# A joined transformer kernel: norm sums, rotation and gate bias moved off GpSimd, rotary tables made earlier, attention issued in steps

## The chip, the cores and the metric

One core of one Trainium2 chip runs the whole program. The metric is device time in microseconds (us) for one execution. Three runs of the kernel before took 2554.97 to 2559.99 us, median 2557.75 us.

## The reference

Two blocks are joined, on one sequence of 512 tokens of width 1024. Block 1 puts 16 meta tokens ahead (528 rows) and runs a gated feed-forward (width 2816), a hybrid mixer, and a second feed-forward. Block 2 runs a recurrent mixer ("hy": an RG-LRU beside an mLSTM in chunks), a convolutional feed-forward (width 3072), a gated embedding ("ple"), then sliding-window attention with rotary positions ("swa"), again a convolutional feed-forward and ple. Each part begins with an RMS norm.

```python
def hybrid_mixer(u, ...):
    sb_q, sb_k, sb_v, c_q, c_kv, k_r, gate_pre = jnp.split(up @ w_in, idx, axis=-1)
    y_sb = from_heads(stick_breaking_attention(sb_q, sb_k, sb_v)) @ w_sb_o   # 8 heads of 64
    q = einsum(rmsnorm(c_q, q_norm_g), w_uq); kv = einsum(rmsnorm(c_kv, kv_norm_g), w_ukv)
    y_mla = from_heads(latent_attention(q_nope, q_rope, k_nope, k_rope, v, cid)) @ w_mla_o
    g = sigmoid(gate_pre + b_gate)
    return (g_sb * y_sb + g_mla * y_mla) @ w_out

def stick_breaking_attention(q, k, v):       # per block of 128 queries
    z = q @ k.T * scale
    log_1m = where(strict, log_sigmoid(-z), 0); csum = cumsum(log_1m)
    a = where(strict, exp(log_sigmoid(z) + csum[..., -1:] - csum), 0)
    return a @ v

def rglru_mlstm_mixer(h, ...):
    y_rg = rg_lru(causal_dwconv(x_rg), ...) * gelu(g_rg)
    q, k = split(silu(causal_dwconv(concat([q, k]))))
    y_ml = sigmoid(o) * rms_norm(mlstm_chunkwise(q, k, v, i_pre, f_pre))
    return concat([y_rg, y_ml]) @ w_out
```

## The kernel before

Activations lie transposed, features on the 128 partitions and tokens along the free side. Every linear layer keeps float32 accuracy by splitting both operands into a high and a low part of type fp32r: `wload` (L280) fetches a weight block of up to 128x1024, ScalarE casts it (`whi`, L286), VectorE subtracts to get the rest (`wlo`, L287), and `mm` (L295 to L302) issues three matmuls per 128 rows, high x high, high x low and low x high. A block of 1024 rows and 512 tokens is thus 24 matmuls of 128x512; these stand at L301 (with L314 for token-major products and L328 for the first products behind a norm). Such a matmul is called a dense matmul below.

A list scheduler sets the order of each engine's instructions, from the order of the code, its priorities (`high_priority`) and its own estimates; each engine then works through its list in order, and the tiles' dependences become semaphore waits. PSUM in the attention stages has four banks for scores (`z`), two for linear layers (`l`) and two for transposes and outputs (`a`).

The mixer of block 1 has two attentions of 8 heads. `stick` (L681) works in four rounds c of two heads: projections of the next round's q and k (`proj`), four gate blocks (`gates`, 96 dense matmuls), and four query blocks b of 128. For each: scores (L717 for two heads at once, L677 for one) plus a mask product with a bf16 identity (L719, L679), a chain of softplus, running sum and exp on ScalarE and VectorE, transposes of the probabilities (L642) and the products with V (L653, `attn_pv`). In L653 each head fills 64 of the 128 output columns, so two heads lie side by side; the last 16 keys are a product of their own with 16 rows. Gates get their bias on GpSimd (L701). `latent` (L751) has the same form with ordinary softmax; its projections are smaller, and the output product of the first attention (`wo`, 96 dense matmuls) follows at its end. Then `mixer` adds the two gated branches on GpSimd (L616), splits and multiplies with `wout`.

`norm` (L388) sums the squares of 8 feature blocks; with `dense=True` all on VectorE, else blocks 1 to 5 on GpSimd (L412). Five norms are not dense: norm_ffn0, norm_ple0, norm_mix1, norm_ffn1 and norm_ple1.

In `hy` (L863) the z of q and k are convolved (L929 to L933), then the gate rows `gts` are scanned and transposed (L956), `weights` (L961) builds the decay matrix of a head from a row sent through DRAM, multiplies it with a causal mask on GpSimd and with q k products (L973, L974), `heads` (L977) makes the head's output, and `rglru` (L1014) runs in the same loop. The output product `hyo` follows with all 8 row blocks.

In `swa` (L1161) `tables` (L1129) computes cosine and sine from the positions at the start, and `norm(g)` in it normalizes and rotates q and k: per half one product with the cosine (`ra`) on VectorE and one with the sine (`rb`) on GpSimd (L1229), and their sum or difference.

Of the kernel before, what the change touches and what calls it, by code (L numbers as in the profile page):

```python
# [15 lines left out]
P = 128  # L16
# [56 lines left out]
def prep(inp):  # L73
# [31 lines left out]
    r["hyo"] = _wt(a["hy_w_out_2"][0].reshape(KD, P, D)[[4, 5, 0, 1, 2, 3, 6, 7]].reshape(D, D))  # L105
# [110 lines left out]
class Kern:  # L216
# [63 lines left out]
    def wload(self, src, n):  # L280
# [4 lines left out]
        with self.tc.high_priority(offset=100):  # L285
# [31 lines left out]
    def lin_first(self, srcs, x, kc, c0=0, wide=False, two=False, k0=0):  # L317
# [12 lines left out]
        return [e if two else e[0][0] for _, e in out]  # L330

# [56 lines left out]
    def norm(self, hs, gname, tt, side, upd=None, tb=P, dense=False):  # L388
# [58 lines left out]
    def begin(self, st):  # L447
# [9 lines left out]
        self.per = self.pool(st, "per")  # L457
        self.pdram = [self.tc.dram_tile([P, KD, T], F32, name=f"pd{l}") for l in range(2)]
# [11 lines left out]
    def ffn(self, n, h, tt, name):  # L470
# [24 lines left out]
        for gi, fh in enumerate((8, 7, 7)):  # L495
# [26 lines left out]
            f0 += fh  # L522
        return self.post(fs, half, hs, tt)

    def mixer(self, n, h):
# [15 lines left out]
        with ExitStack() as stS:  # L541
            S = self.pool(stS, "S")
            vt = S.tile([P, 5, 512], F32, name="sbv")
            with ExitStack() as st:
# [53 lines left out]
            self.stick(S, x, n.rs, vt, ysb, masks[:, :P], gs, gm)  # L598
        n.st.close()
        n.st = ExitStack()  # L600
        for m in range(0, KD, 2):
            self.act(gs[:, m:m + 2, :], gs[:, m:m + 2, :], AF.Sigmoid)
            self.act(gm[:, m:m + 2, :], gm[:, m:m + 2, :], AF.Sigmoid)
        O = self.pool(n.st, "O1")
        ymla = [O.tile([P, 4, T], F32R, name=nm) for nm in ("ymh", "yml")]
        with ExitStack() as st:
            self.latent(st, cq, ckv, kr, masks[:, P:], ymla, ysb, gs)
# [21 lines left out]
    def attn_pv(self, pool, probs, c, nb, vt, ydst, b):  # L629

        nc = self.nc
        hp = ExitStack()
        hp.enter_context(self.tc.high_priority(offset=100))
        slots = [(i, hh) for i in range(nb) for hh in range(2)] + [(nb, hh) for hh in range(2)]
        where = {}
        for g0 in range(0, len(slots), 4):
            grp = slots[g0:g0 + 4]
            pt = self.sbank()
            at = pool.tile([P, 512], F32, name="at", bufs=3)
            for j, (i, hh) in enumerate(grp):  # L640
                kk = P if i < nb else META
                nc.tensor.transpose(pt[:kk, j * P:(j + 1) * P], probs[hh][:, i * P:i * P + kk], self.ident)  # L642
                where[(i, hh)] = at[:kk, j * P:(j + 1) * P]
            n1 = sum(1 for i, hh in grp if i < nb)
            if n1:
                (nc.vector.tensor_copy if (g0 // 4) % 2 else nc.scalar.copy)(at[:, :n1 * P], pt[:, :n1 * P])
            if n1 < len(grp):
                nc.vector.tensor_copy(at[:META, n1 * P:len(grp) * P], pt[:META, n1 * P:len(grp) * P])
        po = self.sbank()[:, :P]
        for i in range(nb + 1):  # L650
            kk = P if i < nb else META
            for hh in range(2):
                nc.tensor.matmul(po[64 * hh:64 * hh + 64, :], vt[:kk, i, (2 * c + hh) * 64:(2 * c + hh + 1) * 64],  # L653
                                 where[(i, hh)], start=i == 0, stop=i == nb)
        sl = slice(b * P, (b + 1) * P)
        nc.scalar.copy(ydst[0][:, c, sl], po)
        self.tt(ydst[1][:, c, sl], po, ydst[0][:, c, sl], ALU.subtract)
        hp.close()

    def units(self):  # L660

        for b in range(4):
            n = META + (b + 1) * P
            for heads in (((0, 1),) if n <= 272 else ((0,), (1,))):
                z = self.psp["z"].tile([P, 2, 512], F32, name="z", tag="z")
                if n <= 512:
                    yield b, heads, n, z[:, :len(heads), :n], [[(z[:, i, :n], 0, n)] for i in range(len(heads))]
                else:
                    w = n // 2
                    yield b, heads, n, z[:, :, :w], [[(z[:, s, :w], s * w, (s + 1) * w) for s in range(2)]]  # L670

    def scores(self, pieces, q, k, mask):

        nc = self.nc
        for i, (ps, a, b) in enumerate(pieces):
            last = i == len(pieces) - 1
            nc.tensor.matmul(ps, q, k[:, a:b], start=True, stop=not last)  # L677
            if last:
                nc.tensor.matmul(ps[:, b - a - P:], self.idb, mask, start=False, stop=True)  # L679

    def stick(self, S, x, rs, vt, ysb, mask, gs, gm):  # L681
# [3 lines left out]
        qk = {}  # L685

        def proj(c):
            q = S.tile([P, T], F32, name="sbq", bufs=2)
            k = S.tile([P, TM], F32, name="sbk", bufs=2)
            ps = self.lin1(d["sbq"][c], x, KD, META)  # L690
            nc.vector.scalar_tensor_tensor(q, ps, 0.125, rs[:, META:], op0=mul, op1=mul)
# [704 lines left out]
```

## Time and profile before

| what | value |
|---|---|
| profiled execution's own time | 2557.62 us |
| its span, mean granted clock | 2555.8 us, 0.997 |
| PE busy / weight loads | 2516.6 us (98%) / 2085.1 us (82%) |
| VectorE / ScalarE / GpSimd busy | 1363.4 (53%) / 974.4 (38%) / 238.4 us (9%) |
| PE on the chain that ended last | 91% |
| DMA | 239.42 MB, mean 94 GB/s |

PE's matmuls are pipelined: a row of the profile shows how long one was in flight, and the next begins before it ends. The pace is read from the distance between the starts, or from the count of matmuls in a stretch. A busy share near 100% can therefore hide a slow pace.

### The profile page before, as it was taken

Reading aid. Unit: us, or ns where it says so; the run is one execution under the profiler, and the core shown is the slowest. Engines: PE = TensorE matmul, PEld = TensorE weight load, DVE = VectorE, ACT = ScalarE, POOL = GpSimd, SP = SyncE. Lnnn points to the kernel's source line nnn. Section 1 sums busy time; section 2 is a strip of 40 time slices with the busy share of each in tenths; the row PEclk is TensorE's granted clock in tenths of the full one; section 3 lists DMA queues with packets and bytes.
Section 4 is the critical chain, followed back from the end, with each engine's and each line's share of the span. In section 5 each row is a group of like instructions: output and inputs, shape, how many; then the busy total and the mean of one; then the engine's idle time right before and its main releaser. Section 6 shows DMA issues by size and latency. Waiting matters only on the chain.

```text
span 2555.8 us, 33215 instructions
## 1 busy us (share of the span) xinstructions
PE 2516.6 (98%) x13328; PEld 2085.1 (82%) x13334; DVE 1363.4 (53%) x2167; ACT 974.4 (38%) x1561; POOL 238.4 (9%) x207
## 2 busy tenths in 40 slices
PE   8999999999999999999999999999999999999999
PEld 8999998767767888888777788888888568888887
DVE  5333347355575542344688655355475776535544
ACT  4222235343663532223534633223343563322332
POOL 1101100011102010101000111001111011100110
PEclk9999999999999999999999999999999999999999
DMA  4222233211112433233322322332333123233232
GB/s 142 90 89 91 91 100 129 80 57 59 49 36 79 150 106 99 95 100 103 113 83 91 124 93 93 96 107 90 92 109 100 34 67 134 93 95 107 91 92 99
DMA packets 77490, 239.42 MB, mean 94 GB/s; under 512 B 9172, under 2 KB 11476, under 8 KB 77080
## 3 DMA queue, kind: packets, MB, share of 16 engines
q1 hardware_dynamic: 77336, 237.30, 28.6%
q8 instruction: 105, 1.72, 0.3%
q14 instruction: 49, 0.40, 0.0%
HBM read 225.72 MB, written 8.40 MB: 92 GB/s over the span
## 4 chain that ended last, share of the span: by engine, by line
PE 91%; DVE 4%; ACT 2%; issue 1%; DMA 1%; POOL 1%; SPq 0%; DVEq 0%; POOLq 0%; ACTq 0%
PE l L301 77%; PE l L328 5%; PE a L653 2%; PE z L677 1%; PE l L314 1%; PE a L642 1%; PE s L1302 1%; PE a L382 1%; DVE wlo L287 1%; PE a L367 1%; POOL gm L247 0%; ACT whi L286 0%; ACT e L236 0%; PE a L1330 0%; PE a L1324 0%
## 5 line engine op out<-in xcount | busy, mean ns | idle before, releaser
L286 ACT CAST whi<-wraw 128x1024 fp32r<-128x1024 f32 (+4 forms) x448 | 432.0, 965 | 1090.9 <-PE l L301 889.2
L301 PE MATMUL l<-xh,whi 128*128 128x512 f32 (+3 forms) x2368 | 786.0, 358 | 0.5 <-DVE sbk L247 0.5
L301 PE MATMUL l<-xl,whi 128*128 128x512 f32 (+3 forms) x2368 | 782.0, 356 | 0.0
L301 PE MATMUL l<-xh,wlo 128*128 128x512 f32 (+3 forms) x2368 | 781.7, 356 | 0.0
L287 DVE TENSOR_TENSOR wlo<-wraw,whi 128x1024 fp32r<-128x1024 f32 (+4 forms) x448 | 502.0, 1121 | 274.0 <-ACT whi L286 265.3
L301 PEld LDWEIGHTS l<-xh,whi 128*128 128x128 f32 (+1 forms) x2368 | 421.6, 188 | 67.2 <-issue 5.5
L301 PEld LDWEIGHTS l<-xh,wlo 128*128 128x128 f32 (+1 forms) x2368 | 420.8, 188 | 64.2 <-issue 2.6
L301 PEld LDWEIGHTS l<-xl,whi 128*128 128x128 f32 (+1 forms) x2368 | 421.4, 188 | 63.0 <-issue 2.5
L301 PE MATMUL l<-chh,whi 128*128 128x512 f32 x384 | 149.4, 389 | 0.0
L301 PE MATMUL l<-chl,whi 128*128 128x512 f32 x384 | 149.4, 389 | 0.0
L301 PE MATMUL l<-chh,wlo 128*128 128x512 f32 x384 | 149.4, 389 | 0.0
L301 PE MATMUL l<-hh,wlo 128*128 128x256 f32 (+2 forms) x528 | 140.1, 320 | 0.0
L301 PE MATMUL l<-hh,whi 128*128 128x256 f32 (+2 forms) x528 | 140.0, 319 | 0.0
L301 PE MATMUL l<-hl,whi 128*128 128x256 f32 (+2 forms) x528 | 139.8, 319 | 0.0
L247 POOL TENSOR_TENSOR t<-g,xrs 128x528 f32<-128x528 f32 (+1 forms) x44 | 75.7, 1722 | 634.5 <-ACT g L236 634.5
L247 POOL TENSOR_TENSOR cc<-cc,xrs 128x512 f32<-128x512 f32 x48 | 62.8, 1309 | 602.9 <-ACT cc L236 602.9
L247 DVE TENSOR_TENSOR t<-l,t 128x256 f32<-128x256 f32 (+1 forms) x66 | 32.3, 516 | 147.4 <-PE l L301 143.5
L247 DVE TENSOR_TENSOR g<-l,xrs 128x256 f32<-128x256 f32 (+1 forms) x66 | 32.3, 516 | 118.7 <-PE l L301 114.7
L301 PEld LDWEIGHTS l<-hh,whi 128*128 128x128 f32 x528 | 88.3, 188 | 6.8
L301 PEld LDWEIGHTS l<-hl,whi 128*128 128x128 f32 x528 | 88.1, 188 | 6.9
L301 PEld LDWEIGHTS l<-hh,wlo 128*128 128x128 f32 x528 | 88.1, 188 | 6.9
L247 DVE TENSOR_TENSOR cz<-l,xrs 128x512 f32<-128x512 f32 x48 | 33.2, 692 | 110.0 <-PE l L301 105.5
(341 smaller groups left out, 3192.9 us busy)
## 6 DMA issues: line engine op xcount, KB each, us to landing
wraw<-in_up SPq DMA_DIRECT2D x96, 512.0 KB, 3.4
wraw<-in_dn SPq DMA_DIRECT2D x64, 384.0 KB, 3.1
wraw<-in_ffn_g SPq DMA_DIRECT2D x44, 512.0 KB, 3.4
wraw<-in_ffn_u SPq DMA_DIRECT2D x44, 512.0 KB, 3.4
wraw<-in_ffn_d SPq DMA_DIRECT2D x32, 448.0 KB, 3.2
wraw<-in_hy SPq DMA_DIRECT2D x20, 512.0 KB, 3.5
wraw<-in_ffn_d SPq DMA_DIRECT2D x16, 512.0 KB, 3.4
wraw<-in_gate SPq DMA_DIRECT2D x16, 512.0 KB, 3.4
```

Of the source, the lines that this page charges most:

```text
L247: return (eng or self.nc.vector).tensor_tensor(out, a, b, op=op)
L286: nc.scalar.copy(hi, raw)
L287: nc.vector.tensor_tensor(lo, raw, hi, op=ALU.subtract)
L301: self.nc.tensor.matmul(ps, a[:, k * m:(k + 1) * m], b[:, k0 + k, c0:c1], start=first and k == 0 and pi == 0, stop=last and k == kc - 1 an ...
L314: self.nc.tensor.matmul(ps[:c1 - c0, :n], a[:, k, c0:c1], b[:, j * n:(j + 1) * n], start=k == 0 and pi == 0, stop=k == nk - 1 and pi == 2)
L328: self.nc.tensor.matmul(ps, a[:, k * P:(k + 1) * P], b[:, k0 + k, t0:t1], start=k == 0 and pi == 0, stop=k == kc - 1 and pi == 2)
L367: nc.tensor.matmul(ps[:w, i * 64:(i + 1) * 64], acc[:, c:c + w], self.ones[:, :64], start=True, stop=True)
L382: nc.tensor.matmul(p[:, c - a:c - a + w], r[:w, i:i + 1].to_broadcast([w, P]), self.ident[:w, :w], start=True, stop=True)
L642: nc.tensor.transpose(pt[:kk, j * P:(j + 1) * P], probs[hh][:, i * P:i * P + kk], self.ident)
L653: nc.tensor.matmul(po[64 * hh:64 * hh + 64, :], vt[:kk, i, (2 * c + hh) * 64:(2 * c + hh + 1) * 64], where[(i, hh)], start=i == 0, stop=i ...
L677: nc.tensor.matmul(ps, q, k[:, a:b], start=True, stop=not last)
L1302: nc.tensor.matmul(z[:, i * n:(i + 1) * n], qt[r, 2 * g + i, b * P:(b + 1) * P], kt[r, g, k0:k0 + n], start=False, stop=i == 1)
```

## The change

Linear layers in the two attentions become generators (`step_lin`) which yield after each of a block's dense products, and a loop (`fill`) hands out a set number of them between the parts of an attention; transposes (`attn_t`) and V products (`attn_v`) become two calls with fills between; the last 16 keys lie in a zeroed tile of 128 rows, so that their V product has 128 rows too; scores of two heads are issued in turn; `wo` of the first attention goes into the second. Five norms sum wholly on VectorE, the gates' bias goes into ScalarE's Sigmoid, the last three branch sums and the rotation's `rb` go to VectorE. The rotary tables are made in the second feed-forward, written to DRAM and read in `swa`. In `hy` the gates' scan and `rglru` come before `weights`, first taps and biases go to ScalarE, and `hyo` is two products of four row blocks, the first of them issued between the heads.

```diff
+    def step_lin(self, src, x, kc, done, c0=0, two=False):
+        hi, lo = self.wload(src, kc * P, 2000)
+        segs, ev = self.banks2() if two else self.banks1(c0)
+        for k in range(kc):
+            for pi, (a, b) in enumerate(((hi, x[0]), (hi, x[1]), (lo, x[0]))):
+                for ps, t0, t1 in segs:
+                    self.nc.tensor.matmul(ps, a[:, k * P:(k + 1) * P], b[:, k, t0:t1],
+                                          start=k == 0 and pi == 0, stop=k == kc - 1 and pi == 2)
+                yield
+        with self.tc.high_priority(offset=1000):
+            done(ev)
...
-                self.tt(acc, acc, sq, ALU.add, None if dense or k > KD - 3 else nc.gpsimd)
+                self.tt(acc, acc, sq, ALU.add)
...
+            if not two and gi == 0:
+                with ExitStack() as st:
+                    self.tables(self.pool(st, "trg", side=self.other))
...
-            self.act(gs[:, m:m + 2, :], gs[:, m:m + 2, :], AF.Sigmoid)
+                self.act(g[:, m, :], g[:, m, :], AF.Sigmoid, bias=self.v("b_gate", b + m))
...
-            self.tt(gm[:, m, :], gm[:, m, :], gs[:, m, :], add, nc.gpsimd)
+            self.tt(gm[:, m, :], gm[:, m, :], gs[:, m, :], add, nc.gpsimd if m < 5 else None)
...
+    def last_keys(self, pt, o, probs, nb, rest, where):
+        for hh in range(2):
+            self.nc.tensor.transpose(pt[:META, o + hh * P:o + (hh + 1) * P], probs[hh][:, nb * P:nb * P + META], self.ident)
+            where[(nb, hh)] = rest[:, hh * P:(hh + 1) * P]
+        self.nc.vector.tensor_copy(rest[:META, :], pt[:META, o:o + 2 * P])
...
+        for row in zip(*todo):
+            for hh, (ps, a, b), last in row:
+                nc.tensor.matmul(ps, q(hh), k(hh)[:, a:b], start=True, stop=not last)
...
+        for c in range(4):
+            ng = (3, 4, 4, 5)[c]
+            self.todo = ([proj(c + 1)] if c < 3 else []) + [gates.pop(0) for _ in range(ng)]
+            if c == 0:
+                self.fill(8)
+            probs = start(c, 0)
+            if late:
+                self.attn_v(*late)
+            self.fill(12)
+            for b in range(4):
+                if b < 3:
+                    nxt = start(c, b + 1)
+                    self.fill((14, 18, 22)[b])
+                else:
+                    self.fill(24 * ng + (48 if c < 3 else 0) - (8 if c == 0 else 0) - 102)
+                t = self.attn_t(S, probs, c, b + 1, vt, ysb, b, rest[b % 2])
+                self.fill(6)
...
+        for i, c in enumerate((0, 4, 1, 5, 2, 6, 3, 7)):
+            z = z_of(8 + c)
+            t = R.tile([P, T], F32, name="t", bufs=2)
+            self.conv(t, z, [self.v(f"mlc{j}", c) for j in range(4)])
+            self.act(qk[:, c, :], t, AF.Silu, bias=self.v("mlcb", c))
+            if i % 2:
+                rglru(i // 2)
...
+            if hd > 1:
+                for m in range(4 * hd - 8, 4 * hd - 4):
+                    out(m)
...
-                self.tt(b, xs[1 - s_], sin, mul, nc.gpsimd)
+                self.tt(b, xs[1 - s_], sin, mul)
```

PE in the first attention before, round c = 0, last query block (L642 transposes of the probabilities `e`, L653 products with V, L301 dense matmuls of the gates):

```order
L642 MATMUL a<-cst,e 16x128
L301 MATMUL l<-xh,whi 128x512
L301 MATMUL l<-xl,whi 128x512
L301 MATMUL l<-xh,wlo 128x512
L653 MATMUL a<-at,sbv 64x128
L301 MATMUL l<-xh,whi 128x512
L653 MATMUL a<-at,sbv 64x128
L301 MATMUL l<-xl,whi 128x512
L653 MATMUL a<-at,sbv 64x128
L301 MATMUL l<-xh,wlo 128x512
```

The same block after, round c = 1 (L343 dense, L672 and L684 transposes, L695 V products, `rest` the zeroed tile of the last keys):

```order
L672 MATMUL a<-cst,e 128x128 x6
L343 MATMUL l<-xl,whi 128x512
L343 MATMUL l<-xh,wlo 128x512
L684 MATMUL a<-cst,e 16x128 x2
L343 MATMUL l<-xh,whi 128x512
L695 MATMUL a<-at,sbv 64x128 x8
L695 MATMUL a<-rest_4907,sbv 64x128 x2
L343 MATMUL l<-xl,whi 128x512
```

The ten V products, which stood one by one between dense matmuls in rounds 0 and 1, stand in one row in every round.

PE in `hy` before, from the second transpose of the gate rows to the first decay products (L314 dense, L973 products of q and k):

```order
L314 MATMUL l<-whi,xh 128x512
L956 MATMUL a<-cst,gts 128x4 x4
L314 MATMUL l<-whi,xl 128x512
L314 MATMUL l<-wlo,xh 128x512
...
L973 MATMUL l<-qk 128x512
L973 MATMUL l<-qk 128x384
L973 MATMUL l<-qk 128x256
L973 MATMUL l<-qk 128x128
```

And after (L1075 the transposes, L1090 the products):

```order
L301 MATMUL l<-xh,wlo 128x512
L1075 MATMUL a<-cst,gts 128x4 x8
L314 MATMUL l<-whi,xh 128x512
L314 MATMUL l<-whi,xl 128x512
...
L1090 MATMUL l<-qk 128x512
L1090 MATMUL l<-qk 128x384
L1090 MATMUL l<-qk 128x256
L1090 MATMUL l<-qk 128x128
```

Between the transposes and the first q k product there were 8 dense matmuls, and there are 96 now.

VectorE in `swa`, rotation of the last query group, before (`x` the normalized halves, L1224; `rb` is GpSimd's):

```order
L1224 SCALAR_TENSOR_TENSOR x_16451<-a,vecs,x_16451 128x512
L1224 SCALAR_TENSOR_TENSOR x_16533<-a,vecs,x_16533 128x512
L247 TENSOR_TENSOR ra_16657<-x_16451,trig 128x512
L247 TENSOR_TENSOR ra_16666<-x_16533,trig 128x512
L247 TENSOR_TENSOR ra_16657<-ra_16657,rb_16658 128x512
L247 TENSOR_TENSOR ra_16666<-ra_16666,rb_16667 128x512
```

And after:

```order
L1336 SCALAR_TENSOR_TENSOR x_16509<-a,vecs,x_16509 128x512
L1336 SCALAR_TENSOR_TENSOR x_16591<-a,vecs,x_16591 128x512
L247 TENSOR_TENSOR ra_16715<-x_16509,trig 128x512
L247 TENSOR_TENSOR rb_16716<-x_16591,trig 128x512
L247 TENSOR_TENSOR ra_16724<-x_16591,trig 128x512
L247 TENSOR_TENSOR ra_16715<-ra_16715,rb_16716 128x512
L247 TENSOR_TENSOR rb_16725<-x_16509,trig 128x512
```

The two sine products now stand in VectorE's own list.

## Rows read from the trace of the kernel before

**Rows 1.** Stretches: us, each engine's busy us (instructions), PE clock, DMA share, GB/s
```profile
27.00:398.00 371.00, 371.00 (x3050) 371.00 (x3049) 141.47 (x212) 108.47 (x143) 37.90 (x26) 1.00 0.29 92
501.96:608.86 106.90, 106.67 (x563) 74.47 (x562) 58.44 (x91) 42.55 (x77) 11.43 (x23) 1.00 0.18 60
608.86:683.62 74.76, 74.53 (x416) 51.39 (x415) 49.69 (x80) 46.05 (x81) 11.20 (x20) 1.00 0.16 51
702.93:782.33 79.40, 78.50 (x552) 53.25 (x550) 55.77 (x163) 47.32 (x129) 0.00 (x0) 1.00 0.10 32
900.00:1238.00 338.00, 338.00 (x1494) 279.73 (x1493) 134.98 (x153) 106.67 (x134) 38.12 (x23) 1.00 0.31 100
```
**Rows 2.** The same for the dense matmuls of L301 alone
```profile
501.96:608.86 106.90, 79.77 (x337) 55.78 (x336) 1.00 0.18 60
608.86:683.62 74.76, 51.15 (x193) 34.38 (x192) 1.00 0.16 51
702.93:782.33 79.40, 27.22 (x104) 16.47 (x102) 1.00 0.10 32
```
**Rows 3.** Timeline of PE, round 1: start, us in flight, then what
```profile
588.66 0.43 PE L653 MATMUL a<-at,sbv 128*64 128x128 f32 x2
589.02 0.50 PE L301 MATMUL l<-xh,whi 128*128 128x512 f32 x1
589.45 0.43 PE L653 MATMUL a<-at,sbv 128*64 128x128 f32 x2
```
**Rows 4.** Timeline of PE, round 2
```profile
635.74 1.46 PE L653 MATMUL a<-at,sbv 128*64 128x128 f32 x20
637.13 0.50 PE L301 MATMUL l<-xl,whi 128*128 128x512 f32 x1
```
**Rows 5.** Timeline of PE, round 0, first query block
```profile
508.14 0.44 PE L653 MATMUL a<-at,sbv 128*64 128x128 f32 x4
508.51 0.50 PE L301 MATMUL l<-xh,whi 128*128 128x512 f32 x1
```
**Rows 6.** Timeline of PE, scores of two heads, then of one
```profile
556.25 0.73 PE L717 MATMUL z<-sbk,sbq 64*128 64x272 f32 x4
556.91 0.28 PE L719 MATMUL z<-masks,idb 128*128 128x128 bf16 x2
...
560.21 0.92 PE L677 MATMUL z<-sbk,sbq 64*128 64x400 f32 x2
561.06 0.33 PE L642 MATMUL a<-cst,e 128*128 128x128 f32 x1
```
**Rows 7.** Waits of PE's weight loads, 684 to 783: us in total, times, longest
```profile
PEld a L653 <- ACT at L646: 2.8, 7, 0.6
```
**Rows 8.** Waits of PE, 1340 to 1440
```profile
PE l L973 <- DVE s L974: 2.8, 1, 2.8
PE l L328 <- ACT xh L291: 2.3, 1, 2.3
PE a L1003 <- DVE nm L1002: 2.3, 3, 1.4
PE a L956 <- DVE gts L247: 0.7, 1, 0.7
```
**Rows 9.** Waits of PE, 783 to 880
```profile
PE l L328 <- ACT ooh L291: 2.1, 1, 2.1
```
**Rows 10.** Groups of GpSimd and VectorE by form: busy us, mean ns, idle before
```profile
L247 POOL TENSOR_TENSOR acc<-acc,sq 128x512 f32<-128x512 f32 x25 | 35.6, 1424 | 237.6 <-ACT sq L226 237.6
L247 POOL TENSOR_TENSOR gm<-gm,gs 128x512 f32<-128x512 f32 x8 | 14.7, 1832 | 128.9 <-DVE gm L247 128.9
L287 DVE TENSOR_TENSOR wlo<-wraw,whi 128x1024 fp32r<-128x1024 f32 x306 | 376.0, 1230 | 188.6 <-ACT whi L286 185.2
L247 DVE TENSOR_TENSOR ra<-x,trig 128x512 f32<-128x512 f32 x10 | 14.9, 1518 | 0.0
L247 DVE TENSOR_TENSOR ra<-ra,rb 128x512 f32<-128x512 f32 x10 | 6.4, 679 | 0.0
```

More of the change, by code (lines that the diff above doesn't have):

```diff
@@ L627, in mixer, with attn_t @@
         return h, upd
-    def attn_pv(self, pool, probs, c, nb, vt, ydst, b):
+    def attn_t(self, pool, probs, c, nb, vt, ydst, b, rest):
         nc = self.nc
-        hp = ExitStack()
-        hp.enter_context(self.tc.high_priority(offset=100))
-        slots = [(i, hh) for i in range(nb) for hh in range(2)] + [(nb, hh) for hh in range(2)]
+        slots = [(i, hh) for i in range(nb) for hh in range(2)]
         where = {}
[L636 to L670, printed above, removed]
@@ L672, in scores @@
-    def scores(self, pieces, q, k, mask):
-        nc = self.nc
[L675 to L679, printed above, removed]
+        with self.tc.high_priority(offset=100):
+            for g0 in range(0, len(slots), 4):
+                grp = slots[g0:g0 + 4]
+                pt = self.sbank()
+                at = pool.tile([P, 512], F32, name="at", bufs=3)
+                for j, (i, hh) in enumerate(grp):
+                    nc.tensor.transpose(pt[:, j * P:(j + 1) * P], probs[hh][:, i * P:(i + 1) * P], self.ident)
+                    where[(i, hh)] = at[:, j * P:(j + 1) * P]
+                n1 = len(grp) * P
+                if n1 <= 256:
+                    self.last_keys(pt, 256, probs, nb, rest, where)
+                (nc.vector.tensor_copy if (g0 // 4) % 2 else nc.scalar.copy)(at[:, :n1], pt[:, :n1])
+            if nb % 2 == 0:
+                self.last_keys(self.sbank(), 0, probs, nb, rest, where)
@@ L792, in proj, with qdone @@
-            return qk
-        nxt = proj(0)
-        late = None
-        for c in range(4):
-            qk = nxt
-            if c < 3:
-                nxt = proj(c + 1)
+                    yield from self.step_lin(d["uq"][4 + 2 * j + c // 2], cq, 3, turn(j))
+            qk[c] = [[], []]
+            def qdone(ev):
+                for hh in range(2):
+                    q = L.tile([96, T], F32, name=f"q{hh}", bufs=2)
+                    self.copy(q[:64], ev[0][0][64 * hh:64 * hh + 64])
+                    i = 2 * (c % 2) + hh
+                    self.tt(q[64:96], t12[32 * i:32 * i + 32, 0, :], t12[32 * i:32 * i + 32, 1, :], add)
+                    qk[c][hh].append(q)
@@ new lines, in kdone, with wo, done @@
+            def kdone(ev):
+                for hh in range(2):
+                    k = L.tile([96, TM], F32, name=f"k{hh}", bufs=2)
+                    for p, s in ev:
+                        self.copy(s(k[:64]), p[64 * hh:64 * hh + 64])
+                    self.copy(k[64:96], kr)
+                    qk[c][hh].append(k)
+            yield from self.step_lin(d["uq"][c], cq, 3, qdone)
+            yield from self.step_lin(d["uk"][c], ckv, 2, kdone, two=True)
+        def wo(m):
+            def done(ev):
+                self.tt(gs[:, m, :], ev[0][0], gs[:, m, :], mul)
+            yield from self.step_lin(d["wo"][m][:, :512], ysb, 4, done)
@@ L937, in hy @@
             self.act(sq[:, c, :], sq[:, c, :], AF.Sqrt, bias=tiny)
+        for c in range(4):
+            self.act(rr[:, c, :], rr[:, c, :], AF.Exp, scale=sl[:, c, 1:2])
         L = R2.tile([4, T], F32, name="lf")
```

281 lines of the change are left out of this document (166 added, 115 removed).

## The prediction

> **What bounds the kernel now.** I read the shares of the page first: PE is busy 98% of the span and carries 91% of the chain that ended last, so only PE's list counts, and other engines only where PE waits for them. A busy share says nothing of the pace, so next I compared stretches by PE's count. In the dense stretch 900 to 1238 there are 1494 matmuls in 338 us, 0.226 us each; in 27 to 398, where they have half the width (256 or 272), 3050 in 371 us, 0.1216 each [rows 1]. All feed-forwards run at this pace and the change can give nothing there. The two attentions don't. In rounds 0 and 1 of the first (501.96 to 608.86) L301 has 337 matmuls [rows 2], by the code 240 whole and 97 half ones: 240 x 0.226 + 97 x 0.1216 = 66.1 us. The other 40.8 of 106.9 us are the attention's own products and what they cost around them. Rounds 2 and 3 have 193 whole ones, 43.7 us, and 31.1 us besides. The second attention has 104, 72 whole and 32 half: 20.2 us, and 59.2 besides. Together 131 us go there, and `hy` has 8.1 us of waits of PE [rows 8]. That is where I look.
>
> **The change part by part.**
>
> *First attention.* The four rounds have the same attention work, yet 0 and 1 take 40.8 us and 2 and 3 take 31.1. The timeline shows why: in rounds 0 and 1 the ten V products of the last query block stand singly between dense matmuls. One takes 0.36 us from its start to the next start (588.66 to 589.02), and the dense one behind it 0.43 instead of 0.226 [rows 3]; together 0.56 us above the dense pace. In round 2 the same ten stand in one row and take 1.39 us (635.74 to 637.13) [rows 4]. So 10 x 0.56 - 1.39 = 4.2 us are lost in each of two rounds, 8.4 of the 9.7. The order after shows one row of ten in every round. I take 9, between 8.4 and 9.7. The last keys, a product of 16 rows, now have 128 rows and stand in the row of the others. Two V products by themselves take 0.37 us (508.14 to 508.51) [rows 5], ten 1.39, so two in a row of ten 0.28; a joined row saves 0.09 at least, and 0.3 where a dense matmul behind a V product goes too (0.43 against 0.226) [rows 3]. Of 16 blocks that is 1.4 to 4.8; I take 2.5, near the middle since the rows for both are there. Scores of two heads in turn run side by side: four matmuls of 64x272 begin and end within 0.66 us, while one head of 64x400 takes 0.85 [rows 6]. After, the 400-key scores of both heads are neighbours in rounds 1 and 2 and not in 0 and 3, so up to 0.85 each; I take 1.5. Sum 13 us, from 9 (with 4 us given back to new waits) to 16.
>
> *Second attention.* Its products stay. The same 16 joined rows give 2.5 again (1.4 to 4.8). What else can go is waiting: it has few dense matmuls to put between, and V products wait seven times for the copy behind their transposes, 2.8 us [rows 7]. The 96 dense matmuls of `wo`, which stood behind it, now stand between; they cost the same 21.7 us in either place, but cover these waits. I take 2.5 + 2.8 = 5.3, from 1.4 (waits stay) to 9 (waits of the other kinds go as well, at the upper price for the rows).
>
> *Branch sums.* PE waits 2.1 us for the first split behind the last sum [rows 9]. That sum takes 1.83 us on GpSimd; one of that shape takes 0.68 on VectorE [rows 10], so 1.15 goes on the last block, and a little on the two before: 1.5, from 0.5 to 2.1.
>
> *`hy`.* The wait for `s` (2.8) and for the gate rows (0.7) [rows 8] arise where only 8 dense matmuls, 1.8 us, lie between the transposes of the gate rows and the first products of q and k. There are 96 after, 21.7 us: both go. The waits for `nm` (2.3) come where VectorE has `rglru` in its list between the steps of a head; that work is now ahead of the loop: 2.0 goes. The wait for `xh` (2.3) is for the split before `hyo`; the first half of `hyo` now begins with blocks that come from the gelu, behind the same table load on ScalarE, so I give it 1.3. Sum 6.8, from 3 to 8.1. It doubles the loads of `hyo` to 16 halves and adds 8 additions of 0.68 on VectorE, 5.5 us beside some 43 us of dense matmuls: nothing, and 5.5 if that cover failed.
>
> *Rotation.* Per group VectorE now does 2 x 1.518 + 2 x 0.679 = 4.4 us while GpSimd makes `rb` [rows 10]. With `rb` in its own list it has six instructions. If all go at 0.679, that is 4.1, 0.3 less; if `ra` stays at 1.518, 5.8, 1.4 more. The `ra` and the sum have the same shape and differ by 2.2 times, and only `ra` runs beside GpSimd, so I take the first: five groups, 1.0 us (from -7 to 1.6). The Trainium skill (SBUF — State Buffer, Who interferes with whom) says that a VectorE instruction with two inputs in SBUF contends with a GpSimd instruction that reads SBUF; by that rule `ra` falls back to its own duration, and by a plain count of instructions the change would cost 5 x 2 x 0.68 = 6.8 us here. The rows bear out the rule.
>
> *Norm sums and tables.* A norm's five sums take 5 x 1.424 = 7.1 us on GpSimd and 5 x 0.68 = 3.4 on VectorE [rows 10], 3.7 us less, but behind each norm stand 48 dense matmuls or so (10.9 us) that need no scale. That covers four of the norms; at norm_mix1, where the tables' VectorE instructions stood in front too, I take 1.2 (from 0 to 3.7). The tables move into the second feed-forward: VectorE is busy 135 of 338 us there [rows 1], and their 19 instructions are 13 us at 0.68 each. On SP the DMA that writes them waits for the last Sin with weight loads behind it; two blocks are ahead, 48 dense matmuls, 10.9 us. If that were not enough, PE would lose a few us once.
>
> *Gate bias.* Sixteen GpSimd instructions go; nothing waited for them but Sigmoid, which now is 16 instead of 8 instructions, behind the last gates and beside 77 dense matmuls.
>
> **Sum.** 13 + 5.3 + 1.5 + 6.8 + 1.0 + 1.2 = 28.8 us off the profiled execution's own 2557.6 (span 2555.8 and 1.8 around it; the median of the runs is 2557.75): 2528.8 us.
>
> **The rivals.**
>
> *A: new waits where switches go.* In the order after, a row of V products stands one or two dense matmuls (0.2 to 0.45 us) behind its transposes, and the copy lies between. Rows 7 price such a wait at 0.4 us (2.8 over 7). On 32 blocks that is 12.8 us: 2541.6. For it: the copies stay on ScalarE and VectorE, which are more than half busy here [rows 1]. Against: rounds 2 and 3 have the same form already and are the better ones.
>
> *B: everything at its upper price.* 16 + 9 + 2.1 + 8.1 + 1.6 + 3.7 = 40.5: 2517. For it: the stretches have waits that I did not count; against: all of it at once.
>
> *C: slower.* `step_lin` puts its casts 2000 places ahead where 100 were. ScalarE and VectorE work in order, so a cast and a subtraction of 1.23 us [rows 10] can stand ahead of the softmax of each query block, and each cast waits for a buffer that PE frees. If each of 32 blocks comes 1.23 us late with no cover, 39 us are lost: 2568. It decides from 28.8 / 32 = 0.9 us a block. For it: VectorE is busy 55 to 70% in these stretches [rows 1]. Against: before, too, these casts go ahead of the softmax, and 18 to 39 dense matmuls (4 to 9 us) now stand between scores and transposes of the long blocks.
>
> *D: the order hardly changes.* The call that would hold PE's order by hand is not used; the list scheduler may place the pieces as it did. The order after speaks against it in round 1. Then only the last four terms stay, 10.5: 2547.
>
> **How the numbers follow.** Forecast 0.60, A 0.20, B 0.12, C 0.04, D 0.04. The predicted time is the forecast's 2529, its own range 2522 to 2537 (the first two terms at 16 + 9 or at 9 + 1.4). The range for 8 in 10 takes in A and D and most of B, and leaves C out: 2510 to 2547; its lower end stands below B because waits not counted could go too. A measurement of this kernel can tell about 0.2%, 5 us, from no change. Only C ends above, and a worse D inside: faster 0.93, same 0.03, slower 0.04.
>
> **What would show it.** Right: the first attention's rounds each near 14.5 us above their dense matmuls; V products in rows of ten at 1.24 to 1.4 us; no wait for `s` or `gts` in `hy`; `ra` near 0.68 us; dense stretches unchanged to the microsecond. Wrong: transposes or V products that wait 0.4 us and more in every block (A), or whole-microsecond waits of PE for `e` with casts ahead of it on ScalarE (C); a wait of PE behind SP's write of the tables.

## The result, and the profile after

The kernel after takes 2533.09 us (median of 4 runs, 2530.61 to 2533.38) against 2558.69 us before (4 runs, 2554.97 to 2559.99): ratio 0.990, 95% interval 0.9883 to 0.9917. Forecast 2529, range 2510 to 2547. The total is close; the terms that make it up are not.

The page after: the span, and each engine's busy time and instructions.

```profile
span 2531.4 us, 33257 instructions
PE 2496.9 (99%) x13334; PEld 2081.7 (82%) x13334; DVE 1360.7 (54%) x2197; ACT 993.6 (39%) x1601; POOL 162.3 (6%) x159
```

GpSimd lost 76 us of work and ScalarE gained 19. Of the 24.4 us that the span lost, 6.8 are clock: TensorE lost them to half speed in the profile of before (rows below), and after it lost none until the work ended. The runs differ likewise: their granted clock is 0.995 to 0.998 before (all series) and 0.998 to 1.0 after. Where the 24.4 us went is read from the starts of TensorE's matmuls: between the same two products of both traces, the difference of the distances is the gain of that stage.

| stage, by TensorE's products | before, us | after, us | gain | forecast |
|---|---|---|---|---|
| start to the mixer's first norm product of `rc` | 438.04 | 441.13 | -3.10 | 0 |
| to the first product of `wout` (both attentions) | 380.00 | 374.45 | 5.55 | 18.3 |
| to the last product of `wout` (branch sums) | 47.38 | 45.65 | 1.73 | 1.5 |
| to the first product of `pph` behind feed-forward 2, the norm ahead of it with it | 373.65 | 372.08 | 1.57 | 0 |
| to the first down product (`chh`) of convolutional feed-forward 0, with `hy` | 366.19 | 360.98 | 5.21 | 6.8 |
| to its last down product | 260.89 | 260.89 | 0.00 | 0 |
| to the first down product of feed-forward 1, with norms, ple and `swa` | 378.19 | 364.84 | 13.35 | 2.2 |
| the rest | 306.99 | 306.99 | 0.00 | 0 |

Two rows stand out: the attentions gave 13 us less than forecast, `swa` gave 11 us more. The first row is no effect of the change: TensorE's list is the same there in all fourteen kernels, and the twelve below reach that product 0.26 to 3.53 us later than the profile of before did. About 1.1 of the 3.1 us is there by the 200th product. The rest comes from the pace: from 100 to 200 us the profile of before has 824 matmuls and that of after 819, with no wait and the clock at 1.00 in both. Seven of the twelve run at the pace of after and five at that of before; what sets it is open.

The four rounds of the first attention after, then the second attention: each stretch, its length, and busy time and count of the dense matmuls alone (L343; answers to [rows 2]).

```profile
495.34:537.46 42.12, 29.07 (x137) 22.06 (x136) 1.00 0.20 63
537.46:587.52 50.06, 36.70 (x169) 27.98 (x168) 1.00 0.21 64
587.52:637.85 50.33, 36.69 (x169) 27.95 (x168) 1.00 0.21 64
637.85:678.39 40.54, 27.41 (x107) 19.18 (x106) 1.00 0.10 31
699.70:794.88 95.18, 47.79 (x177) 29.42 (x177) 1.00 0.14 42
```

At 0.2262 us for a whole dense matmul and half of it for a half, the rounds stand 16.8, 17.4, 17.7 and 16.6 us above their dense work, where 14.5 each was forecast. Rounds 0 and 1 together fell from 41 to 34, as the regrouped V products promise, but rounds 2 and 3 rose from 31 to 34. The row of ten is as forecast (answer to [rows 3, 4], round 0):

```profile
535.10 1.09 PE L695 MATMUL a<-at,sbv 128*64 128x128 f32 x16
536.02 0.39 PE L695 MATMUL a<-rest,sbv 128*64 128x128 f32 x4
536.34 0.50 PE L343 MATMUL l<-xh,wlo 128*128 128x512 f32 x1
```

Ten products take 1.24 us (535.10 to 536.34), 1.39 before. What rose are the waits. TensorE's waits from 441 to 816 after (line, releaser: us, times, longest):

```profile
PE a L672 <- ACT e L236: 3.9, 9, 0.7
PE l L343 <- ACT q L243: 3.1, 2, 2.4
PE l L343 <- DVE sbk L247: 2.1, 4, 0.6
PE a L672 <- DVE e L894: 1.1, 1, 1.1
```

and the same stretch before, 438 to 818:

```profile
PE l L301 <- ACT q L243: 1.3, 2, 0.7
PE l L765 <- ACT mlav L243: 0.6, 1, 0.6
PE l L301 <- DVE sbk L247: 0.5, 1, 0.5
PE z L677 <- DVE e L739: 0.4, 2, 0.2
```

2.8 us became 10.2 here. Inside the four rounds alone it is 0.4 before and 5.5 after: 3.9 for `e`, ahead of transposes, and 1.6 for `sbk`.

The scores did not run as forecast either. Two heads' products lie side by side when both start at once. The four records of 64x400 of both heads in round 1 (each product leaves two) did not, though they are neighbours in TensorE's list. The first row is the kernel after; the second and third are two kernels from the experiments below, with casts 100 places ahead and with the first attention's order held by hand:

```profile
549.35 1.97 PE L721 MATMUL z<-sbk,sbq 64*128 64x400 f32 x4
547.81 1.49 PE L721 MATMUL z<-sbk,sbq 64*128 64x400 f32 x4
546.72 0.94 PE L721 MATMUL z<-sbk,sbq 64*128 64x400 f32 x4
```

They take 1.90 us to the next start after, 1.42 and 0.87 in the other two. Over the whole first attention the scores take, from each start to the next and without idle time, 21.8 us before, 20.7 after, 17.9 with casts 100 ahead and 12.4 by hand. Why the second head starts late is not shown.

The largest wait, 2.37 us from 688.8 to 691.1, is for the copy of `q` at the start of the second attention, with this ahead of it on ScalarE:

```profile
684.85 3.18 ACT L236 ACTIVATE gm<-gm,vecs 128x512 f32<-128x512 f32 x5
687.94 1.03 ACT L286 CAST whi<-wraw 128x1024 fp32r<-128x1024 f32 x1
688.87 0.72 ACT L236 ACTIVATE gm<-gm,vecs 128x512 f32<-128x512 f32 x1
...
689.90 0.57 ACT L243 COPY q<-l 64x512 f32<-64x512 f32 x1
```

Six of the sixteen Sigmoids stand there.

In `swa` the trace of before holds what the prediction did not look at. TensorE, with the idle time ahead of a row in brackets:

```profile
1968.33 0.39 PE L301 MATMUL l<-xh,wlo 128*128 128x512 f32 x1
1970.35 1.08 PE L1210 MATMUL a<-hsel,ss 128*128 128x64 f32 x8 [1.63 <-DVE ss L247]
...
1972.37 0.63 PE L301 MATMUL l<-xl,whi 128*128 128x512 f32 x1
1972.79 0.63 PE L301 MATMUL l<-xh,wlo 128*128 128x512 f32 x1
```

and VectorE before, just ahead of that wait:

```profile
1965.28 3.12 DVE L247 TENSOR_TENSOR ra<-x,trig 128x512 f32<-128x512 f32 x2
...
1969.52 0.68 DVE L247 TENSOR_TENSOR ss<-ss,sqa 128x512 f32<-128x512 f32 x1
```

`ss`, which TensorE waits for, stands behind the two slow `ra`. A second wait of 1.68 us follows at 1983, for `e`, behind the next `ra`. A third group, for `e` of L1316, was 2.8 us before and is 0.7 after (L1428):

```profile
PE a L1324 <- DVE e L1316: 2.8, 4, 1.2
PE a L1436 <- DVE e L1428: 0.7, 2, 0.5
```

After each of the first two waits dense matmuls start 0.43 us apart instead of 0.227. The granted clock of before (last three columns: clock, DMA share, GB/s) says why:

```profile
865.00:870.00 5.00, 3.04 (x17) 2.45 (x16) 1.83 (x2) 2.29 (x4) 0.00 (x0) 0.96 0.24 72
870.00:875.00 5.00, 5.00 (x21) 4.33 (x21) 2.25 (x5) 1.41 (x4) 0.00 (x0) 0.70 0.28 111
1970.00:1975.00 5.00, 4.65 (x19) 3.87 (x20) 3.53 (x9) 2.24 (x5) 0.00 (x0) 0.71 0.43 105
1975.00:1980.00 5.00, 5.00 (x29) 3.82 (x29) 1.24 (x3) 0.00 (x0) 0.00 (x0) 0.95 0.33 105
1985.00:1990.00 5.00, 4.94 (x14) 2.55 (x14) 4.92 (x16) 2.28 (x9) 0.00 (x0) 0.57 0.37 90
1990.00:1995.00 5.00, 5.00 (x19) 2.98 (x17) 0.94 (x6) 3.74 (x16) 0.00 (x0) 0.74 0.23 68
```

A stretch of 5 us at clock c loses 5 x (1 - c): 1.7 us behind the wait at 868, 1.7 behind that at 1969 and 3.45 behind that at 1983, 6.85 in all, at the lower of the two levels (1.2 instead of 2.4 GHz). After:

```profile
1955.00:1980.00 25.00, 25.00 (x123) 17.64 (x122) 20.04 (x55) 10.42 (x37) 0.00 (x0) 1.00 0.27 74
```

It is 1.00 from 862 to 872 us too. In the trace after the clock falls only in the last 2.2 us, where the work ends. The Trainium skill (TensorE: Matmul & The Clock Gate, Why this matters for your kernels) says that idle gaps of TensorE between bursts of matmuls bring the lower clock back. It speaks of longer gaps than these: in the trace of before the clock falls behind waits of 1.6 to 2.0 us. The rotation after, on VectorE (answer to [rows 10]: `ra` 1518 ns before):

```profile
L247 DVE TENSOR_TENSOR rb<-x,trig 128x512 f32<-128x512 f32 x10 | 6.9, 686 | 0.0
L247 DVE TENSOR_TENSOR ra<-x,trig 128x512 f32<-128x512 f32 x10 | 6.8, 684 | 0.0
```

`hy` after, TensorE's waits from 1233 to 1594 (answers to [rows 8]):

```profile
PE l L328 <- DVE h L247: 1.6, 1, 1.6
PE a L1120 <- DVE nm L1119: 1.0, 3, 0.4
PE l L1090 <- DVE s L1091: 0.4, 1, 0.4
```

### The profile page after: what moved, and what is told of

Its sections match the earlier page's. It is cut to its first block, busy times and chain, and to the rows that moved or that the text cites. A ratio compares the mean times of both kernels' runs of the same rounds, so it can differ in the third digit from the quotient of the medians.

```text
span 2531.4 us, 33257 instructions
## 1 busy us (share of the span) xinstructions
PE 2496.9 (99%) x13334; PEld 2081.7 (82%) x13334; DVE 1360.7 (54%) x2197; ACT 993.6 (39%) x1601; POOL 162.3 (6%) x159
## 4 chain that ended last, share of the span: by engine, by line
PE 91%; DVE 4%; ACT 3%; issue 1%; DMA 1%; POOL 0%; SPq 0%; ACTq 0%; DVEq 0%
PE l L301 71%; PE l L328 5%; PE l L343 5%; PE l L314 2%; PE z L721 1%; PE a L695 1%; PE a L672 1%; ACT e L236 1%; PE s L1414 1%; DVE wlo L287 1%; ACT whi L286 1%; PE a L408 1%; PE a L393 1%; DMA wraw<-in_hyo 1%; PE a L1442 1%
## 5 line engine op out<-in xcount | busy, mean ns | idle before, releaser
L301 PE MATMUL l<-xh,whi 128*128 128x512 f32 (+3 forms) x2156 | 707.9, 355 | 0.0
L301 PE MATMUL l<-xh,wlo 128*128 128x512 f32 (+3 forms) x2156 | 705.8, 354 | 0.0
L301 PE MATMUL l<-xl,whi 128*128 128x512 f32 (+3 forms) x2156 | 705.5, 354 | 0.0
L301 PEld LDWEIGHTS l<-xh,whi 128*128 128x128 f32 (+1 forms) x2156 | 382.1, 188 | 56.9 <-issue 1.4
L301 PEld LDWEIGHTS l<-xh,wlo 128*128 128x128 f32 (+1 forms) x2156 | 381.9, 188 | 56.6 <-issue 1.0
L301 PEld LDWEIGHTS l<-xl,whi 128*128 128x128 f32 (+1 forms) x2156 | 382.2, 187 | 56.2 <-issue 1.2
L301 PE MATMUL l<-chh,wlo 128*128 128x512 f32 x384 | 149.4, 389 | 0.0
L301 PE MATMUL l<-chl,whi 128*128 128x512 f32 x384 | 149.4, 389 | 0.0
L301 PE MATMUL l<-chh,whi 128*128 128x512 f32 x384 | 149.4, 389 | 0.0
L301 PE MATMUL l<-hh,wlo 128*128 128x256 f32 (+2 forms) x528 | 140.3, 320 | 0.0
L301 PE MATMUL l<-hl,whi 128*128 128x256 f32 (+2 forms) x528 | 140.2, 320 | 0.0
L301 PE MATMUL l<-hh,whi 128*128 128x256 f32 (+2 forms) x528 | 140.1, 319 | 0.0
L301 PEld LDWEIGHTS l<-hh,whi 128*128 128x128 f32 x528 | 88.4, 188 | 6.9
L301 PEld LDWEIGHTS l<-hl,whi 128*128 128x128 f32 x528 | 88.2, 188 | 6.9
L301 PEld LDWEIGHTS l<-hh,wlo 128*128 128x128 f32 x528 | 88.3, 188 | 6.8
```

Of the source, the lines that this page charges most:

```text
L301: self.nc.tensor.matmul(ps, a[:, k * m:(k + 1) * m], b[:, k0 + k, c0:c1], start=first and k == 0 and pi == 0, stop=last and k == kc - 1 an ...
```

## The experiments

Times are medians; the intervals are of the ratio to before, whose median was 2558.6 to 2559.7 in these series. For the attentions a second figure is given, read as above: time from the first score to the first product of `wout`, less its dense matmuls at 0.2262 us. It is 135.1 before and 130.0 after; a fall of the clock in it counts. A difference of a few us between two single profiles can be clock alone: the wait for `acc` at the norm of feed-forward 2 (1.96 us) is in all fourteen, and behind it the clock costs nothing in five, 1.7 us in seven and 3.4 in two.

### The rotation and the tables

```diff
 # before
-                self.tt(b, xs[1 - s_], sin, mul, nc.gpsimd)
+                self.tt(b, xs[1 - s_], sin, mul)
```

> The kernel before with one edit: rb, the sine product of the rotation, on VectorE instead of GpSimd. Theory (after the two traces were compared): in the second block's attention TensorE waited 1.63 us for ss and 1.68 us for e behind VectorE's slow ra, and after each wait the granted clock stood near 0.5 for about 3.5 and 6.5 us, which costs half of that again; 3.3 + 1.4 + 3.2 = 8 us go, so about 2550.5 against 2558.5, with ra at 0.68 us and clock 1.00 throughout that stage. Rival (the prediction's term): only VectorE's shorter list counts, 1.0 us, about 2557.5.

Measured: 2550.24 us, 0.9969 (0.9957 to 0.9982), 9.5 us faster. `ra` takes 684 ns, both waits are gone, the clock in that stage is 1.00, and the stage is 11.8 us shorter. This one edit is worth 9.5 us, as the theory said; the prediction gave it 1.0.

```diff
 # after
-                self.tt(b, xs[1 - s_], sin, mul)
+                self.tt(b, xs[1 - s_], sin, mul, nc.gpsimd)
```

> The changed kernel with that one edit undone: rb on GpSimd again. Theory: ra goes back to about 1.5 us, TensorE waits behind it again once or twice for 1.5 us, and the clock falls behind each wait: 4 to 8 us, about 2537 to 2541 against 2533. Rival (the prediction's term): 1.0 us, 2534. Third possibility: the tables made elsewhere already shortened that place, then no wait comes back and the time stays at 2533.

Measured: 2541.57 us, 0.9933 (0.9921 to 0.9946), 8.5 slower than after, a little more than the theory's 4 to 8. `ra` is back at 1509 ns, and so are the waits:

```profile
PE s L1410 <- ACT e L236: 1.7, 1, 1.7
PE a L1322 <- DVE ss L247: 1.6, 1, 1.6
PE a L1436 <- DVE e L1428: 2.8, 4, 1.2
```

The stage is 7.3 us longer than after, though in this profile the clock stayed up behind the waits, against the theory:

```profile
1955.00:1965.00 10.00, 8.38 (x42) 6.41 (x40) 7.13 (x14) 2.24 (x5) 0.85 (x1) 1.00 0.38 103
1965.00:1975.00 10.00, 8.33 (x46) 5.63 (x45) 9.08 (x22) 3.07 (x12) 2.54 (x2) 1.00 0.12 31
```

So of the 7.3 us 5.4 are waits (1.7, 1.6, and 2.8 where it was 0.7); the other 1.9 are not traced. The clock's 1.7 + 3.45 came on top in the profile of before: 12.4 by this sum, 11.8 in the kernel above.

```diff
 # after
-            if not two and gi == 0:
-                with ExitStack() as st:
-                    self.tables(self.pool(st, "trg", side=self.other))
...
+            self.tables(tp, trig)
```

> The changed kernel with the rotary tables made at the start of the second block's attention again, as before, and not written to memory. Theory: they carry little of that stage's gain; TensorE loses up to 1.3 us at the norm in front and nothing behind it: 2533 to 2535. Rival: the tables carry the gain of that stage (13 us between its first and last product), so 2540 or more, with waits of TensorE in that stage.

Measured: 2533.67 us, 0.9902 (0.9889 to 0.9916): 0.6 slower than after, no difference that can be told. Its stage is 1.6 us longer than after's, the term of 1.2. Behind it is a wait at the norm, which is in the trace of before (first row), not in that of after, and here again (second row):

```profile
PE a L382 <- DVE xrt L373: 1.1, 1, 1.1
PE a L408 <- DVE xrt L399: 1.4, 1, 1.4
```

The norm's sums are on VectorE here, so by themselves they do not remove it.

### The attentions

> The changed kernel with both attentions of block 1 issued as before (whole linear layers, one head's scores at a time, last keys as a product of 16 rows, the first output product behind the second attention); the gates' bias stays in the Sigmoid. Theory (from the traces): the new order saves 11.8 us in the attentions' own products and gives 7 back in waits of TensorE for exp, q and sbk among the dense products; undoing it costs 4 to 6 us: 2537 to 2539. Rival (the prediction): 18 us, 2551.

The edit puts `stick`, `latent`, `units`, `scores` and `attn_pv` of before back. Measured: 2536.78 us, 0.9914 (0.99 to 0.9927), 3.7 slower than after; above dense 134.4. The whole new order of both attentions is worth 4 to 5 us, as the theory said, not 18.

```diff
-            where[(nb, hh)] = rest[:, hh * P:(hh + 1) * P]
+            where[(nb, hh)] = rest[:META, hh * P:(hh + 1) * P]
...
+                kk = P if i < nb else META
...
-                    nc.tensor.matmul(po[64 * hh:64 * hh + 64, :], vt[:, i, (2 * c + hh) * 64:(2 * c + hh + 1) * 64],
+                    nc.tensor.matmul(po[64 * hh:64 * hh + 64, :], vt[:kk, i, (2 * c + hh) * 64:(2 * c + hh + 1) * 64],
```

> The changed kernel with the V product of the last 16 keys taken over 16 rows again instead of a zero-filled tile of 128, in the same places. The prediction gave the joined rows 2.5 us in each attention, 5 in all. Theory: a row of ten took 1.39 us before and takes 1.24 now, one of four 0.37 in both, so 0.15 on the longest and less on the others, 32 blocks: 2 to 4 us slower than 2533. Rival (upper price of the prediction, a switch of 0.3 us each): 9 us slower. Third: the number of rows is nothing to TensorE: no difference.

Measured: 2538.64 us, 0.9919 (0.9906 to 0.9933), 5.5 slower; above dense 134.9, of it 1.9 more in the first attention, 2.2 in the second and 0.8 between them, where this profile has a fall of the clock. A row of ten takes 1.39 again:

```profile
534.09 1.09 PE L696 MATMUL a<-at,sbv 128*64 128x128 f32 x16
535.12 0.43 PE L696 MATMUL a<-rest,sbv 16*64 16x128 f32 x4
535.48 0.50 PE L343 MATMUL l<-xh,wlo 128*128 128x512 f32 x1
```

The joined rows are worth about 4 us, a little more than the theory's 2 to 4 at most and near the two terms of 2.5. Undoing the whole new order costs hardly more (4 to 5), so all the rest of it together came to next to nothing.

```diff
-        hi, lo = self.wload(src, kc * P, 2000)
+        hi, lo = self.wload(src, kc * P)
```

> The changed kernel with the weight casts of the attentions' dense blocks 100 places ahead instead of 2000. It tests whether the new waits of TensorE in the attentions (3.9 us for e before transposes, 3.1 for q, 2.1 for sbk) come from casts that stand ahead of the softmax on ScalarE and VectorE. Theory: they don't; in the block at 549 to 559 us the chain from scores to exp takes 6.2 us whatever the casts do, and 17.5 dense matmuls (4 us) and a row of V products lie beside it; so within 1 us of 2533, with the waits for e still there. Rival: the casts cause them; then about 5 us go, 2528. Third: casts that come later than needed make TensorE wait for the weights; slower.

Measured: 2530.19 us, 0.9885 (0.9868 to 0.9901), 2.9 faster than after; above dense 126.9. A miss between theory and rival: the waits for `e` stay (3.9 us, 10 of them), but rounds 0 to 2 are 0.6 to 1.4 us shorter each, and the wait for `q` falls from 2.4 to 1.4. What is shorter in the first attention is the scores, by 2.8 us (20.7 to 17.9), because more of them overlap. So casts far ahead cost 3 us, but not by the softmax that rival C has them delay.

```diff
-                self.act(g[:, m, :], g[:, m, :], AF.Sigmoid, bias=self.v("b_gate", b + m))
+            self.act(gs[:, m:m + 2, :], gs[:, m:m + 2, :], AF.Sigmoid)
...
+                nc.gpsimd.tensor_scalar(dst, dst, self.v("b_gate", m), 1.0, op0=add, op1=mul)
```

> The changed kernel with the gates' bias added on GpSimd again and 8 Sigmoids of two blocks instead of 16 of one. Theory: TensorE's wait of 2.37 us for q at the start of the second attention comes from the 16 Sigmoids, six of which stand ahead of the copy of q on ScalarE; 8 of 0.95 us instead of 16 of 0.64 free 2.6 us there, so the wait falls below 1 us and the time by 1.5 to 2.4 us: about 2531. Rival (the prediction: nothing waits for them): no difference, 2533.

Measured: 2531.57 us, 0.9893 (0.9878 to 0.9908), 1.5 faster, which is within the scatter of the runs. The wait for `q` falls from 2.4 to 1.6 us, not below 1, and the time from the mixer's norm to `wout` by 0.4: the direction of the theory, half its size or less.

```diff
-                    self.copy(q[:64], ev[0][0][64 * hh:64 * hh + 64])
+                    (self.nc.scalar.copy if c else self.nc.vector.tensor_copy)(q[:64], ev[0][0][64 * hh:64 * hh + 64])
```

(the copies of `k` likewise)

> The changed kernel with the copies of q and k of the second attention's first two heads on VectorE, which has about 3 us free there, instead of ScalarE, which works through the Sigmoids. Theory: the same wait of 2.37 us for q goes from the other side, and with it the half-speed clock that followed it in two of the profiles: 2530.5, on some runs 2529. Rival: the wait moves to the next copy in ScalarE's list (the keys' turned part or the values), and nothing is won: 2533.

Measured: 2537.12 us, 0.9914 (0.9899 to 0.9929), 4 slower. TensorE now waits 3.4 us for `q` from VectorE instead of 2.4 from ScalarE, and the clock falls behind it (0.73 from 690 to 695). Neither theory nor rival said that. The copies stand in VectorE's list behind two subtractions (1.70 us) that waited 0.85 us for their cast on ScalarE. Of the 4 us the wait explains no more than 1 and the fall behind it 1.7: this profile loses 6.9 us to the clock, also at 818 and 866 us, where the edit changes nothing, and the time from the mixer's norm to `wout` is 1.8 longer than after's.

```diff
-            if True:
+            with self.by_hand():
                 self.stick(S, x, n.rs, vt, ysb, masks[:, :P], gs, gm)
```

> The changed kernel with TensorE's order in the first attention held as the code is written, instead of the list scheduler's. As written 22 dense matmuls stand between the last scores and the transposes of the third block, where the scheduler leaves 17.5 and TensorE waits up to 0.9 us for e. Theory: the scheduler's estimate of the exp chain is what places the transposes too early, so the waits for e in this attention (about 4 us with those for sbk) go: 2529 to 2530. Rival: the written order has its own waits, since a score waits for its bank until the exp two blocks back is done, and each block loses 0.5 us or more: 2537 or above.

Measured: 2526.4 us, 0.9873 (0.9858 to 0.9888), 6.7 faster than after; above dense 124.3. The rounds stand 13.3, 15.6, 15.6 and 15.2 us above dense, near the forecast's 14.5, and no wait for `e` in this attention is left. But 3.8 us for `sbq` are new,

```profile
PE l L343 <- DVE sbq L746: 3.2, 3, 1.2
```

(the three inside the rounds), and the waits inside the rounds are 6.5 us in all, where after has 5.5. So the theory's cause is not what the gain came from, and the gain is twice what it allowed. It is the scores: by hand most of both heads' products start at once, and they take 12.4 us instead of 20.7.

> The version before this one in the list with TensorE's order of the second attention held as written too. As written, 5 dense matmuls lie between scores and transposes there, 1.1 us, and the softmax chain takes longer. Theory: there the scheduler's order is the better one, since there are few dense matmuls to put between, and TensorE waits in each of 16 blocks: 5 us or more slower than without it. Rival: it is as good as in the first attention: 1 to 3 us faster than without it.

The edit, on top of the next kernel: `with self.by_hand():` around `self.latent(...)`. Measured: 2533.21 us, 0.9897 (0.9883 to 0.9911), 9.7 slower than without it; above dense 132.2. TensorE waits 5.4 us for `q` and 2.6 for `k` there, seven waits and not one in each block as the theory had it, and 3.4 us are clock. What the hand wins in one attention it loses in the other.

```diff
+            with self.by_hand():
...
-        hi, lo = self.wload(src, kc * P, 2000)
+        hi, lo = self.wload(src, kc * P)
...
+        for m in range(KD):    # behind self.latent(...)
+            self.act(gm[:, m, :], gm[:, m, :], AF.Sigmoid, bias=self.v("b_gate", KD + m))
```

> A version made of what the runs so far showed: the changed kernel with TensorE's order of the first attention held as written (7 us faster by itself), the attentions' weight casts 100 places ahead (3 us), and the eight Sigmoids of gm behind the second attention instead of ahead of it, so that ScalarE reaches the casts and copies of its first projection 5 us earlier. Theory: TensorE's waits at the start of the second attention (2.4 us for q, or 3.4 for t in the run by hand) go, with the half-speed clock behind them, and the Sigmoids behind it lie beside dense products: 2520 to 2523. Rival: the two attentions' gains overlap and the late Sigmoids are waited for at the first branch sum (8 x 0.64 = 5 us and a table load of 1.3): 2526 to 2530.

Measured: 2523.56 us (2521.7 to 2526.65), 0.9863 (0.9848 to 0.9878); above dense 120.7. It beats both kernels, after by 9.5 us, 0.6 above the theory's range. Its waits between the two attentions, 671 to 692:

```profile
PE l L343 <- DVE t L247: 0.9, 1, 0.9
PE l L343 <- ACT q L243: 0.8, 1, 0.8
```

and the Sigmoids behind the second attention cost nothing that shows.

### `hy`

> The changed kernel with the recurrent mixer hy as before (gate scan behind the convolutions, rglru between the heads, the output product in one piece). Theory: the traces show TensorE's waits between the first gate product and the norm behind hy at 9.2 us before and 4.4 after, and the stage 5.2 us shorter; undoing it costs 5 us: 2538. Rival (the prediction): 6.8 us, 2540, since every wait it named goes; the new wait for h at the norm (1.6 us) would then have another cause.

The edit puts `hy`, `conv` and the row order of `hyo` back. Measured: 2541.26 us, 0.993 (0.9918 to 0.9943), 8.2 slower than after. In its profile the stage is 6.0 us longer than after's, 1.7 of them a fall of the clock at 1420 to 1430; the waits for `nm` (2.3), `xh` (2.4) and `s` (1.8) are back. Another 3.4 us are a fall of the clock at 864, ahead of `hy`, behind the wait for `acc`, which the edit doesn't touch. So `hy` is worth 4.3 us at full clock, 5.2 by the first two traces: the theory's 5, somewhat under the term of 6.8. Its parts were not undone one by one.

## Why the prediction was right, and where it was not

**The total** was 4 us off by luck: 12.7 us too much for the attentions and 11.1 too little for `swa` cancelled.

**First attention, 13 us: failed.** Rows of ten take 1.24 us as forecast, and the joined rows are worth about 4 in both attentions. The step that failed is the one that took rounds 2 and 3 as proof that this form has no waits ("rounds 2 and 3 have the same form already and are the better ones"). The order after has them: 5.1 us more inside the rounds, so the first attention gained 4.2. Rival A was right that waits come, but not about which: transposes wait for `e`, nine times here. The waits that A priced, of the V products' weight loads for the copy, are 7.0 us before and 7.2 after in both attentions together. (ScalarE, by A "more than half busy", is busy 40% in rounds 0 and 1, [rows 1].) The term for the scores (1.5) came to 1.1, and not where it was put, the 400-key scores. It was the larger chance: kept together by hand they save 9.4 us.

**Second attention, 5.3: failed by 3.** Inside it 2.3 us were won, and 1.2 lost at its start. The joined rows came (2.2). The waits for the copy behind the transposes, 2.8 us of the term, did not go; the weight loads' row after (answer to [rows 7]):

```profile
PEld a L695 <- ACT at L677: 3.6, 10, 0.5
```

The scores in turn, no part of the term, gave 2.7 there (21.2 to 18.5 us, as read above); what took as much back is not shown.

**Gate bias: failed.** "Nothing waited for them but Sigmoid" counted who waits for the Sigmoids, not who stands behind them in ScalarE's list: the copy of `q` does, and TensorE waits 2.4 us for it, 0.8 of it for the Sigmoids by the run that undid them.

**Rival C** said that casts 2000 ahead cost time, and they do, 3 us. Its mechanism did not show: the waits for `e` are the same with casts 100 ahead.

**Branch sums (1.5; 1.73 in the trace, not undone alone) and `hy` (6.8; 4.3 to 5.2 at full clock):** right in kind, `hy` a little high. In `hy` the wait for `s` went from 2.8 to 0.4 and that for `gts` to nothing; `nm` gave 1.3 instead of 2.0; the wait for `xh` gave way to one for `h` (1.6), at the norm behind the last additions.

**Rotation, 1.0: failed, by 8 us.** The mechanism was right (`ra` fell to 0.684 us because GpSimd no longer reads beside it). The rule of the Trainium skill (SBUF — State Buffer, Who interferes with whom) held in both directions, 0.684 and 1.509 us. The size was not: it was summed as VectorE's saved time, a list in which 0.3 us a group is nothing, instead of looking for the waits of TensorE behind it. They stood in the trace (1.63, 1.68 and, for `e` of L1316, 2.8 us), with clock 0.57 to 0.74 behind the first two. Its own sum gives five times 0.3, 1.6 us, and why it took 1.0 is not said. The half-speed clock was no term at all, though the span's mean of 0.997 said that some 7 us of 2555.8 were lost to it.

**Norms and tables, 1.2:** right: undoing the tables lengthens the stage by 1.6, and no wait stands behind SP's write. It is the tables; that the norm sums gave anything is not shown.

The 1.57 us at the norm of feed-forward 2 are the clock too: TensorE waits 2.0 us for `acc` there in both traces, and only before did the clock fall behind it.

## What to carry to other kernels

Sum a change from the waits of the engine that bounds, not from the time saved on the engine that is edited: list those waits over the whole span and ask which the edit touches. Where the mean granted clock is under 1, find the stretches that pull it down; the wait ahead of each can cost more than its own length. An instruction made cheaper for one engine and put into another's list delays whatever stands behind it there. Where an order is to bring two heads' products side by side, look at their starts in the trace: the scheduler may leave them apart, as here.

## What the runs showed of the hardware

- A wait of TensorE of 1.3 to 3.4 us is sometimes followed by a few us at half clock and sometimes not, at the same place of the same program text: behind `acc` (2.0 us) in nine of the fourteen profiles, behind the 1.6 and 1.7 us in `swa` in before and not in the kernel with `rb` back on GpSimd. Each fall cost 1.7 or 3.4 us. The Trainium skill (TensorE: Matmul & The Clock Gate, What's actually happening) says that the point at which the clock rises from its low level varies between executions; in these traces it varies too whether it falls at all.
- A stretch without waits can repeat exactly between kernels: 260.89 us for a convolutional feed-forward in both, 0.01 us apart at most in all fourteen traces. It need not: from the 500th to the 3000th product of the first stage, the same list in all, TensorE takes 304.26 us in six profiles and 306.00 in eight, without a wait and at clock 1.00. With its start, that stage scatters by 3.5 us.
- Products of two heads with 64 rows each run side by side when both start at once: four records of 64x400 in 0.87 us, 1.90 where the second head started late.
- Products of 16 rows in a row of products of 128 cost more than products of 128 rows in their place: 1.39 against 1.24 us for ten.
